# Hybrid layer on one core: banks of the down projection read by ScalarE, the residual added by transfers, and keys by token scaled ahead of the chains

## Chip, core and metric

The kernel runs on one core of a Trainium2 chip, in one launch. The metric is the device time of one execution in microseconds (us), lower is better. It took 1257.34 us, the median of three runs (1256.65 to 1259.51).

## What is computed

Input and output are 1024 tokens of 1024 floats. One layer has two mixers beside each other, a gated delta rule (4 heads) and a dilated windowed attention (8 heads), then an output projection, a gated MLP with a short convolution, and a last RMS norm. Cut to what matters here:

```python
h = rmsnorm(x, norm1_w);  proj = h @ w_in
# mixer A, per head and chunk: k is normed by l2norm, g = log decay, beta = sigmoid
k_end = kc * (jnp.exp(gc[..., -1:] - gc) * bc)[..., None]     # keys scaled by token
def step(state, xs):
    u = uv - jnp.einsum('bhck,bhkv->bhcv', wk, state)
    o = jnp.einsum('bhck,bhkv->bhcv', qd, state) + jnp.einsum('bhcj,bhjv->bhcv', at, u)
    state = ge[..., None, None] * state + jnp.einsum('bhck,bhcv->bhkv', ke, u)
    return state, o
x = x + jnp.concatenate([o_a, o_b], axis=-1) @ w_out
h = rmsnorm(x, norm2_w)
u = causal_dwconv(h @ w_up, ffn_conv_w)
gate, up = u[..., :D_FF], u[..., D_FF:]        # D_FF = 2816
x = x + (jax.nn.silu(gate) * up) @ w_down
return rmsnorm(x, final_norm_w)
```

## The kernel before

**Products.** Everything is float32. A product is made of three matmuls in the fp32r type (`mm3`, line 184): each operand is split into a high part (ScalarE, a copy that rounds) and a low part (VectorE, the difference), as in `split_block` (1052). So each operand of each product costs one ScalarE and one VectorE instruction. All matmuls have the line of `mm` (L177) in the profile and transposes that of `tp` (L181). All instructions of VectorE (DVE), ScalarE (ACT), GpSimd (POOL) and the transfers that SP issues have the line of the helper class `Engine` (L132), so groups are told apart by the names of their tiles.

**Order of the work.** The kernel is written as streams (Python generators: projections, keys, chains, attention, MLP), and a planner, `Weave` (lines 46 to 109), interleaves them. It keeps a modelled time of TensorE and of each engine, and resumes the stream that is due (`need` gives the delay after which a tile should be ready). Each TensorE instruction gets an order stamp, so TensorE keeps the planner's order; a scheduler places the instructions of the other engines by their data, so they may come earlier or later than their text. `after` (173) adds a wish on that order. A change of an operation's engine or cost in one stream can so move other streams' products.

**Keys of the delta rule** (`kprep`, 524; four heads, before 130 us). For each head, rows of log decay come into `dec`, ScalarE adds a bias in 8 instructions, GpSimd masks, ScalarE takes the exponential. TensorE transposes the keys `kT` to keys by token; `tokens` (505) copies them to `ktok` with ScalarE and adds up the squares of each chunk (`sq`, result `ssk`). From `ssk`, `beta` and `eg` come the 8 factors by chunk, `bp` and `ke`. Then TensorE multiplies keys by keys (`ps<-kT`), VectorE scales the result to `um`, which goes to the triangular solve.

**Chains** (`chain`, 730; four, from about 232 to 297 us, beside projection products). In a chunk, TensorE makes the 128x128 product `ps[:, P:2P]`; VectorE writes it scaled by `ke` into `wke`, and ScalarE copies it unscaled into `w`. `ktok` times `wke` gives the step of the state (read by VectorE), `at` times `w` the output.

**Down projection** (lines 1241 to 1411, from about 1027 us to the end). It is a Strassen-Winograd product of 2 x 2 halves: seven products of half size in four stages. Stages 0, 1 and 2 do two products each, stage 3 one. A stage has 11 steps j (`STEPS`, 1361), one for each pair of 128 rows of weights. A step multiplies four weight tiles of 128 columns by activations of 512 tokens for each product: into the four PSUM banks `pa` and the four `pb`, 24 matmuls in all. Banks accumulate over the steps, and partly over the stages. When a stage ends (j = 10) all eight banks are read: `add_to` (1329) lets VectorE add a bank to a half of an output row block `x1h[m]`, m = 0 to 7. `ADDS` (1364) says which. The first products of the next stage write the same banks. The step (1, 4) is step 4 of stage 1.

`prep` (1279) makes the operands of the next step while this one runs. SP loads raw weights (`wd`, `wa`, 512 and 256 KB). In stage 0 the activations come from `upark` in DRAM into `r1`. VectorE forms the weight sums in place, ScalarE and VectorE split them into tiles `pr`. The activations' sums T1 to T4 of the algorithm stay in `r1` and `r2`: T1 is formed in stage 0; T2 in a tile `t2` and T4 in stage 1; T3 in stage 2. `load_x1` (1315) loads the residual from `xpark` in 16 transfers of 256 KB on SP, at the steps in `XLOADS` (1362).

**Last norm.** `complete` (1333) squares a finished block on ScalarE and adds the squares to `rstdB` on VectorE. `final_norm` (1342) adds them over the partitions with matmuls against ones, takes the power on GpSimd, spreads it by transposes and scales eight blocks on VectorE, with a transfer of each to the output. `last_product` (1397) does the last five steps of stage 3 for one bank and half of its tokens at a time.

Of the kernel before, what the change touches and what calls it, by code (L numbers as in the profile page):

```python
# [135 lines left out]
def hybrid_layer(tc, I, out):  # L136
# [387 lines left out]
    def kprep(h):  # L524
# [29 lines left out]
        bp = small("bp", 4)  # L554
        ve.reciprocal(bp, ssk)
        ve.tensor_tensor(bp, bp, beta[:, :, h], op=OP.mult)
        ke = small("ke", 4)
        ve.tensor_tensor(ke, bp, eg, op=OP.mult)

        um = A("um", "uy", shape=(P, NCH, P))  # L560
        for c0 in range(0, NCH, 4):
# [12 lines left out]
        d.update(kT=kT, dec=dec, ge=ge, nk=nk, bp=bp, ke=ke, um=um)  # L574
        wv.done.add(("k", h))
        if all(("k", i) in wv.done for i in range(H)):
            forward_sub()
# [152 lines left out]
    def chain(h):  # L730
# [2 lines left out]
            yield from wv.until(("m", i))  # L733
            yield from wv.until(("v", i))
        d = G[h]
        kT, ktok, vtok, yt, ge, rq, gq, ke = [d[n] for n in ("kT", "ktok", "vtok", "yt", "ge", "rq", "gq", "ke")]
        if not ct:
            ct.append(A("ct", "uy", shape=(P, 8, P)))
        sts = ct[0][:, 2 * h:2 * h + 2, :]
# [5 lines left out]
        for c in range(NCH):  # L745
            cs = slice(c * P, (c + 1) * P)
            if c == 2 and h < 2:
                qb = chain_load(h, 1)
            if c == 3 and h >= 2:
                yield from wv.until(("c", h - 2, 3))  # L750
                qb = chain_load(h, 1)
            if c == 4:
                qa = qb
            qT, at = [qa[:, i, (c % 4) * P:(c % 4 + 1) * P] for i in range(2)]
            if c == 0:
                r = vtok[:, cs]
                yield wv.need(ps, vtok, yt)
            else:
                yield wv.need(ps, st, slack=HOP)
                mm(ps[:, 0:P], kT[:, cs], st, 0.215)  # L760
                r = tile_(sp, [P, P], F32, "r", "r" + tg, 1)
                ve.scalar_tensor_tensor(r, ps[:, 0:P], ngam[:, c, h:h + 1], vtok[:, cs], op0=OP.mult, op1=OP.add)
                yield wv.need(r, slack=HOP)
            mm(ps[:, P:2 * P], yt[:, c, :], r, 0.215)
            w = tile_(sp, [P, P], F32, "w", "w" + tg, 1)
            if c < NCH - 1:
                wke = tile_(sp, [P, P], F32, "wke", "r" + tg, 1)
                ve.tensor_scalar(wke, ps[:, P:2 * P], ke[:, c:c + 1], None, op0=OP.mult)
# [282 lines left out]

    def split_block(b, src):
        ac.activation(b[0], src, AF.Copy)
        ve.tensor_tensor(b[1], src, b[0].bitcast(F32), op=OP.subtract)

    def residual(m):

# [186 lines left out]
    x1h = {}  # L1244
    pcount = [0]
    LAST = 5

    def raw_tile(name, tag, src, n=2):
        t = tile_(wp, [P, n, 512], F32, name, tag, 2)
# [12 lines left out]
    def split_pair(src):  # L1262
# [4 lines left out]
        split_block((hi[0], lo[0]), src)  # L1267
        return [(hi[0][:, i, :], lo[0][:, i, :]) for i in range(2)]

    def split_one(src, tag=None):  # L1270
        if tag is None:
# [7 lines left out]
    def prep(stage, j):  # L1279
        if stage == 0:  # L1280

            g = raw_tile("wd", ("wst", "whi")[j % 2], wd_rows(j, 0))
            r = R1[j] = acts("r1", R1TAGS[j], j, 0)
            ops[stage, j] = list(zip(split_pair(g), split_pair(r)))
            q = R2[j] = A("r2", R2TAGS[j], shape=(P, 2, 512))
            sy.dma_start(q[:, 0, :], upark[j][:, half(1)])
            ve.tensor_tensor(r[:, 0, :], q[:, 0, :], r[:, 0, :], op=OP.subtract)
        elif stage == 1:

            u = raw_tile("wd", "wst", wd_rows(j, 1))  # L1290
            a = raw_tile("wa", "whi", wd_rows(j, 0)[:, 0:1], 1)
            r, q = R1[j], R2[j]
            sy.dma_start(q[:, 1, :], upark[HT + j][:, half(1)])
            t2 = tile_(wp, [P, 512], F32, "t2", "wlo", 2)
            ve.tensor_tensor(u[:, 1, :], u[:, 0, :], u[:, 1, :], op=OP.add)
            ve.tensor_tensor(u[:, 0, :], u[:, 1, :], a[:, 0, :], op=OP.subtract)
            ve.tensor_tensor(t2, q[:, 1, :], r[:, 0, :], op=OP.subtract)
            w = split_pair(u)
            ops[stage, j] = [(w[0], split_one(t2)), (w[1], split_one(r[:, 0, :]))]
            ve.tensor_tensor(r[:, 1, :], r[:, 1, :], t2, op=OP.subtract)  # L1300
        elif stage == 2:

            g = raw_tile("wd", "wst", wd_rows(j, 0))
            u = raw_tile("wd", "whi", wd_rows(j, 1))
            ve.tensor_tensor(g, g, u, op=OP.subtract)
            ve.tensor_tensor(g[:, 1, :], g[:, 0, :], g[:, 1, :], op=OP.add)
            r = R2[j]
            ve.tensor_tensor(r[:, 0, :], r[:, 1, :], r[:, 0, :], op=OP.subtract)
            ops[stage, j] = list(zip(split_pair(g), split_pair(r)))
        else:  # L1310

            a = raw_tile("wa", ("wst", "whi")[j % 2], wd_rows(j, 1)[:, 1:2], 1)
            ops[stage, j] = [(split_one(a[:, 0, :]), split_one(R1[j][:, 1, :], R2TAGS[j]))]

    def load_x1(mg, hh):
        for m in range(4 * mg, 4 * mg + 4):
            if not hh:
                x1h[m] = A("x1h", ("kT", "kT", "dv", "dv", "Xa", "Xa", "Xa", "Xa")[m])
            sy.dma_start(x1h[m][:, half(hh)], xpark[m][:, half(hh)])

    def down(pd, i, op, sl, first, last_):
        (whi, wlo), (hhi, hlo) = op
# [10 lines left out]
    def complete(m, hh, sl):  # L1333

        sp_ = part(m, hh, sl)
        x = x1h[m][:, sp_]
        sq = tile_(sp, [P, 512], F32, "sq3", "t2", 2)
        ac.activation(sq[:, sl] if m else rstdB[:, sp_], x, AF.Square)
        if m:
            ve.tensor_tensor(rstdB[:, sp_], rstdB[:, sp_], sq[:, sl], op=OP.add)  # L1340

    def final_norm(hh, sl, tags, between=None):
        n_ = (sl.stop - sl.start) // P
        ss = bank(tags[0])
        for c in range(n_):
            o = 512 * hh + sl.start + c * P
            mm(ss[:, c:c + 1], rstdB[:, o:o + P], ones[:, :1], 0.215)
# [8 lines left out]
        for m in range(8):  # L1356
            x = x1h[m][:, part(m, hh, sl)]
            ve.scalar_tensor_tensor(x, x, fw[:, m:m + 1], pb[:, :sl.stop - sl.start], op0=OP.mult, op1=OP.mult)
            sy.dma_start(out[m * P:(m + 1) * P, part(m, hh, sl)], x)

    STEPS = [(s_, j) for s_ in range(4) for j in range(HT)]
    XLOADS = {6: (0, 0), 12: (1, 0), 14: (0, 1), 16: (1, 1)}

    ADDS = (((0, 0), (0, 0)), ((0, 1), (1, 1)), ((1, 1), (0, 1)))

    def mlp_down():
        yield from wv.until("up")
# [3 lines left out]
        def down_step(stage, j):  # L1371
            for e, (op, pds) in enumerate(zip(ops[stage, j], (pa, pb))):
                for i in range(4):
                    down(pds[i], i, op, whole, j == 0 and (stage == 0 or (stage, e) == (1, 1)), j == HT - 1)
                if j == HT - 1:
                    mg, hh = ADDS[stage][e]
                    for i in range(4):
                        add_to(pds[i], 4 * mg + i, hh, whole)
                        if stage == 0 and e == 1:
                            complete(i, 0, whole)  # L1380
                        if stage == 2 and e == 1:
                            complete(i, 1, whole)
                    if stage == 2 and e == 1:
# [3 lines left out]
        for n, (stage, j) in enumerate(STEPS):  # L1387
            if n + 1 < len(STEPS):
                prep(*STEPS[n + 1])
            if n in XLOADS:  # L1390
                load_x1(*XLOADS[n])
# [5 lines left out]
        def last_product(i, sl):  # L1397
# [3 lines left out]
            complete(4 + i, 0, sl)  # L1401


        left, right = slice(0, 256), slice(256, 512)
# [81 lines left out]
```

## Time and profile before

| what | value |
|---|---|
| time, median of 3 runs | 1257.34 us |
| profiled execution: time, span | 1259.56 us, 1257.8 us |
| TensorE busy | 1233.0 us, 98% |
| VectorE busy | 936.0 us, 74% |
| ScalarE busy | 621.8 us, 49% |
| GpSimd busy | 47.8 us, 4% |
| mean granted TensorE clock | 0.993 |
| moved by transfers | 153.52 MB, mean 122 GB/s |

In the lines of the timeline, the first number is the start, the second the time from there to the end of the group, and the bracket tells how long the engine was idle before it and whose work ended that. In the list of waits, a row gives the sum, the number of times and the longest. In the windows, the numbers are the window's length, then the busy time and instruction count of TensorE, its weight loads, VectorE, ScalarE and GpSimd, then the granted clock, the share of the DMA engines and GB/s. A releaser is inferred, and a product that waits for several things is put down to the last.

### The profile page before, as it was taken

What the parts mean: (1) busy time and instruction counts of PE and PEld (TensorE: products, weight loads), DVE (VectorE), ACT (ScalarE), POOL (GpSimd) and SP (SyncE); (2) the same over time, 40 slices, a digit from 0 to 9 for tenths busy, and PEclk for the clock granted to TensorE, in tenths of its full rate; (3) what the DMA queues carried; (4) which work ended last, traced back from release to release, by engine and by line L of the source; (5) the groups of instructions that cost most, each with busy time, mean ns of one, the idle gap of its engine ahead of it and who ended that gap; (6) DMA issues with size and microseconds to landing.
All of it is one profiled execution on the core that took longest, in us unless ns stands there. A gap on an engine that the chain in (4) does not pass through costs nothing.

```text
span 1257.8 us, 18320 instructions
## 1 busy us (share of the span) xinstructions
PE 1233.0 (98%) x7040; PEld 1002.1 (80%) x7040; DVE 936.0 (74%) x1462; ACT 621.8 (49%) x1179; POOL 47.8 (4%) x34
## 2 busy tenths in 40 slices
PE   9989999999999999999999999999999999999996
PEld 7768887888676767878788888888888888787886
DVE  7566975563555455676798888888988989899875
ACT  7374444462757374465554454544544454343451
POOL 0021110022000000000000000000000000000000
PEclk9989999999999999999999999999999999999998
DMA  6313244255223420454312313223223298545523
GB/s 228 100 57 94 85 116 137 101 160 206 96 78 100 140 63 26 126 179 139 118 51 101 92 59 101 85 67 101 79 73 101 68 353 290 167 138 198 192 85 134
DMA packets 81974, 153.52 MB, mean 122 GB/s; under 512 B 21824, under 2 KB 32736, under 8 KB 81888
## 3 DMA queue, kind: packets, MB, share of 16 engines
q1 hardware_dynamic: 81888, 152.37, 37.1%
q8 instruction: 55, 0.90, 0.3%
q14 instruction: 31, 0.25, 0.1%
HBM read 114.31 MB, written 35.93 MB: 119 GB/s over the span
## 4 chain that ended last, share of the span: by engine, by line
PE 84%; DVE 7%; DMA 4%; ACT 2%; issue 2%; SPq 0%; POOL 0%; POOLq 0%; DVEq 0%; ACTq 0%
PE ps L177 44%; PE pa L177 18%; PE pc L177 9%; PE dw L177 8%; PE ps L181 4%; DMA wd<-in_wd 3%; DVE pr L132 2%; DVE x1h L132 1%; DVE wd L132 1%; ACT dec L132 1%; DVE kT L132 1%; PE warm L177 1%; DMA wst<-in_wu 0%; DVE r L132 0%; DVE xr L132 0%
## 5 line engine op out<-in xcount | busy, mean ns | idle before, releaser
L177 PE MATMUL dw<-pr 128*128 128x512 f32 (+1 forms) x984 | 213.3, 377 | 2.8 <-DVE x1h L132 2.8
L177 PEld LDWEIGHTS dw<-pr 128*128 128x128 f32 x984 | 176.1, 188 | 38.9 <-DVE x1h L132 4.9
L177 PE MATMUL ps<-xhi,whi 128*128 128x512 f32 x448 | 186.5, 416 | 0.0
L177 PE MATMUL ps<-xhi,wlo 128*128 128x512 f32 x448 | 175.8, 392 | 0.0
L177 PE MATMUL ps<-xlo,whi 128*128 128x512 f32 x448 | 175.3, 391 | 0.0
L177 PE MATMUL pa<-T,pair 128*128 128x512 f32 x528 | 127.1, 389 | 0.6 <-ACT u L132 0.6
L177 PEld LDWEIGHTS pa<-T,pair 128*128 128x128 f32 x528 | 99.0, 188 | 21.1 <-ACT u L132 0.7
L177 PEld LDWEIGHTS ps<-xhi,whi 128*128 128x128 f32 x448 | 84.6, 189 | 19.9 <-issue 6.0
L177 PEld LDWEIGHTS ps<-xhi,wlo 128*128 128x128 f32 x448 | 84.4, 188 | 18.5
L177 PEld LDWEIGHTS ps<-xlo,whi 128*128 128x128 f32 x448 | 84.8, 189 | 13.5
L132 ACT ACTIVATE sm<-sm,mx 128x512 f32<-128x512 f32 (+2 forms) x128 | 79.9, 651 | 23.0 <-DVE mx L132 23.0
L132 ACT ACTIVATE u<-pa 128x512 f32<-128x512 f32 x44 | 26.4, 600 | 110.5 <-PE pa L177 110.5
L132 DVE SCALAR_TENSOR_TENSOR y<-xu,fcw,y 128x1023 f32<-128x1023 f32 (+1 forms) x44 | 56.3, 1281 | 25.7 <-ACT y L132 25.7
L132 ACT ACTIVATE whi<-wst 128x1024 fp32r<-128x1024 f32 (+2 forms) x38 | 38.7, 1017 | 70.4 <-PE ps L177 63.0
L177 PE MATMUL pc<-B,pair 128*128 128x512 f32 x264 | 63.4, 389 | 0.0
L177 PE MATMUL pa<-B,A 128*128 128x512 f32 x264 | 63.4, 389 | 0.0
L177 PE MATMUL pc<-T,S 128*128 128x512 f32 x264 | 63.4, 389 | 0.0
L177 PE MATMUL pa<-T,S 128*128 128x512 f32 x264 | 63.4, 389 | 0.0
L132 ACT ACTIVATE pr<-wd 128x1024 fp32r<-128x1024 f32 x33 | 35.0, 1061 | 55.0 <-DVE wd L132 36.5
L132 DVE TENSOR_TENSOR wst<-wst 128x512 f32<-128x512 f32 x88 | 60.5, 687 | 0.7
L177 PE MATMUL ps<-B,pair 128*128 128x512 f32 x252 | 60.5, 389 | 0.0
L177 PEld LDWEIGHTS pc<-B,pair 128*128 128x128 f32 x264 | 49.6, 188 | 10.3
(230 smaller groups left out, 2279.8 us busy)
## 6 DMA issues: line engine op xcount, KB each, us to landing
wst<-in_wu SPq DMA_DIRECT2D x44, 512.0 KB, 3.7
wd<-in_wd SPq DMA_DIRECT2D x44, 512.0 KB, 4.3
wst<-in_wi SPq DMA_DIRECT2D x25, 512.0 KB, 3.7
upark<-y SPq DMA_DIRECT2D x22, 512.0 KB, 3.7
apark<-aqkv SPq DMA_DIRECT2D x12, 512.0 KB, 2.8
r<-upark SPq DMA_DIRECT2D x11, 512.0 KB, 7.6
r<-upark SPq DMA_DIRECT2D x22, 256.0 KB, 6.7
wa<-in_wd SPq DMA_DIRECT2D x22, 256.0 KB, 2.9
```

What stands on the lines that cost most here:

```text
L132: return getattr(eng, op)(*a, **kw)
L177: tc.stamp_issue_order_token(nc.tensor.matmul(dst, lhs, rhs, start=start, stop=stop, **kw).ins, TOKEN)
L181: tc.stamp_issue_order_token(nc.tensor.transpose(dst, src, ident).ins, TOKEN)
```

## The change

Five things change.

1. Down projection: at the ends of stages 0 and 1 ScalarE copies the banks into `x1h` (`copy_to`). The two products of stage 0 now go to two row blocks, `x1h[i]` and `x1h[4 + i]`, and `add_half` lets VectorE add the second to the first in steps 13 to 16. At the end of stage 2 VectorE adds banks as before.
2. The residual: `add_res` issues 12 transfers of 256 KB on GpSimd's queue that add a DRAM block to `x1h` in place (`accum_op`). Four plain loads by SP are left. The squares of the first four half blocks, once made at the end of stage 0, are made at steps 24 to 29 (`JOBS`), though the scheduler may place them earlier.
3. Activations' sums: stage 0 loads both halves of `r2` in one transfer and forms T3, and for j of 5 or more (`LATE`) T4. Stage 1 forms T2 in place, without the tile `t2`. Weight sums are asked to come behind the previous weights' split (`weight_sum`).
4. Last norm: the squares of the last two blocks are not added to `rstdB` but are summed by more matmuls into the same PSUM column (`more`).
5. Keys: `ktok` is scaled by `ke` once, by seven ScalarE instructions of 128x128 for each head. In the chain, VectorE copies the product into `w`, which both following products use; `wke` and ScalarE's copy are gone.

In the list of instructions, ScalarE has 756 rows in place of 778 and VectorE 1315 in place of 1306. TensorE's order is that of before up to 283 rows (the products up to the second head's keys), differs in how the projection's products lie between the third and fourth heads' key products, and is the same in the chains.

```diff
@@ kprep @@
-        ke = small("ke", 4)
+        ke = small("ke")
         ve.tensor_tensor(ke, bp, eg, op=OP.mult)
+        for c in range(NCH - 1):
+            ac.activation(v8(d["ktok"])[:, c, :], v8(d["ktok"])[:, c, :], AF.Copy, scale=ke[:, c:c + 1])
@@ chain @@
+            ve.tensor_copy(w, ps[:, P:2 * P])
             if c < NCH - 1:
-                wke = tile_(sp, [P, P], F32, "wke", "r" + tg, 1)
-                ve.tensor_scalar(wke, ps[:, P:2 * P], ke[:, c:c + 1], None, op0=OP.mult)
-            ac.activation(w, ps[:, P:2 * P], AF.Copy)
-            if c < NCH - 1:
-                yield wv.need(wke, slack=HOP)
-                mm(ps[:, 2 * P:3 * P], ktok[:, cs], wke, 0.215)
+                yield wv.need(w, slack=HOP)
+                mm(ps[:, 2 * P:3 * P], ktok[:, cs], w, 0.215)
@@ prep, stage 0 @@
-            ops[stage, j] = list(zip(split_pair(g), split_pair(r)))
-            q = R2[j] = A("r2", R2TAGS[j], shape=(P, 2, 512))
-            sy.dma_start(q[:, 0, :], upark[j][:, half(1)])
+            ops[stage, j] = list(zip(weight_pair(g), split_pair(r)))
+            q = R2[j] = acts("r2", R2TAGS[j], j, 1)
             ve.tensor_tensor(r[:, 0, :], q[:, 0, :], r[:, 0, :], op=OP.subtract)
+            ve.tensor_tensor(q[:, 0, :], q[:, 1, :], q[:, 0, :], op=OP.subtract)
+            if j >= LATE:
+                ve.tensor_tensor(r[:, 1, :], r[:, 1, :], q[:, 1, :], op=OP.subtract)
+                ve.tensor_tensor(r[:, 1, :], r[:, 1, :], r[:, 0, :], op=OP.add)
@@ prep, stage 1 @@
-            sy.dma_start(q[:, 1, :], upark[HT + j][:, half(1)])
-            t2 = tile_(wp, [P, 512], F32, "t2", "wlo", 2)
-            ve.tensor_tensor(u[:, 1, :], u[:, 0, :], u[:, 1, :], op=OP.add)
+            weight_sum(u[:, 1, :], u[:, 0, :], u[:, 1, :], op=OP.add)
             ve.tensor_tensor(u[:, 0, :], u[:, 1, :], a[:, 0, :], op=OP.subtract)
-            ve.tensor_tensor(t2, q[:, 1, :], r[:, 0, :], op=OP.subtract)
-            w = split_pair(u)
-            ops[stage, j] = [(w[0], split_one(t2)), (w[1], split_one(r[:, 0, :]))]
-            ve.tensor_tensor(r[:, 1, :], r[:, 1, :], t2, op=OP.subtract)
+            w = weight_pair(u)
+            t1 = split_one(r[:, 0, :])
+            ve.tensor_tensor(r[:, 0, :], q[:, 1, :], r[:, 0, :], op=OP.subtract)
+            ops[stage, j] = [(w[0], split_one(r[:, 0, :])), (w[1], t1)]
+            if j < LATE:
+                ve.tensor_tensor(r[:, 1, :], r[:, 1, :], r[:, 0, :], op=OP.subtract)
@@ prep, stage 2 @@
-            ve.tensor_tensor(r[:, 0, :], r[:, 1, :], r[:, 0, :], op=OP.subtract)
@@ new helpers @@
+    def weight_sum(*a, **kw):
+        inst = ve.tensor_tensor(*a, **kw)
+        if wlast[0] is not None:
+            after(inst, wlast[0], "raw weights are released before the next ones are waited for")
+    def add_res(mg, hh):
+        for m in range(4 * mg, 4 * mg + 4):
+            po_.dma_start(x1h[m][:, half(hh)], xpark[m][:, half(hh)], accum_op=OP.add)
+    def add_half(m):
+        x = x1h[m][:, half(0)]
+        in_turn(x, x, x1h[4 + m][:, half(0)])
+    def copy_to(pd, m, hh):
+        ac.activation(x1h[m][:, half(hh)], pd, AF.Copy)
@@ final_norm @@
+        parts = [rstdB[:, o:o + n_ * P]] + list(more)
+        for i, t in enumerate(parts):
+            for c in range(n_):
+                mm(ss[:, c:c + 1], t[:, c * P:(c + 1) * P], ones[:, :1], 0.215, i == 0 and c == 0,
+                   i == len(parts) - 1, skip_group_check=True)
@@ the order of the jobs @@
-    XLOADS = {6: (0, 0), 12: (1, 0), 14: (0, 1), 16: (1, 1)}
-    ADDS = (((0, 0), (0, 0)), ((0, 1), (1, 1)), ((1, 1), (0, 1)))
+    ADDS = (((0, 0), (1, 0)), ((0, 1), (1, 1)), ((1, 1), (0, 1)))
+    JOBS = {6: [(take_x1, 0)], 8: [(take_x1, 1)], 13: [(add_half, 0)], 14: [(add_half, 1)], 15: [(add_half, 2)],
+            16: [(add_half, 3)], 17: [(add_res, 0, 0)], 19: [(load_x1, 1, 0)], 24: [(add_res, 0, 1), (square, 0)],
+            25: [(square, 1)], 26: [(add_res, 1, 1)], 27: [(square, 2)], 29: [(square, 3)]}
@@ mlp_down @@
-                        add_to(pds[i], 4 * mg + i, hh, whole)
-                        if stage == 0 and e == 1:
-                            complete(i, 0, whole)
+                        if stage < 2:
+                            copy_to(pds[i], 4 * mg + i, hh)
+                        else:
+                            add_to(pds[i], 4 * mg + i, hh, whole)
@@ the end @@
-        for i in (2, 3):
-            last_product(i, right)
-        final_norm(0, right, ("hf", "ch"))
+        final_norm(0, right, ("hf", "ch"), more=[last_product(i, right, True) for i in (2, 3)])
```

More of the change, by code (lines that the diff above doesn't have):

```diff
@@ L573, in kprep @@
             sy.dma_start(md[r], um[b, :, b])
-        d.update(kT=kT, dec=dec, ge=ge, nk=nk, bp=bp, ke=ke, um=um)
+        d.update(kT=kT, dec=dec, ge=ge, nk=nk, bp=bp, um=um)
         wv.done.add(("k", h))
@@ L735, in chain @@
         d = G[h]
-        kT, ktok, vtok, yt, ge, rq, gq, ke = [d[n] for n in ("kT", "ktok", "vtok", "yt", "ge", "rq", "gq", "ke")]
+        kT, ktok, vtok, yt, ge, rq, gq = [d[n] for n in ("kT", "ktok", "vtok", "yt", "ge", "rq", "gq")]
         if not ct:
@@ L1053, in split_block @@
         ac.activation(b[0], src, AF.Copy)
-        ve.tensor_tensor(b[1], src, b[0].bitcast(F32), op=OP.subtract)
+        return ve.tensor_tensor(b[1], src, b[0].bitcast(F32), op=OP.subtract)
     def residual(m):
@@ L1246, in hybrid_layer @@
     LAST = 5
+    LATE = 5
     def raw_tile(name, tag, src, n=2):
@@ L1260, in acts, with weight_pair, split_pair @@
         return t
-    def split_pair(src):
+    wlast = [None]
+    def weight_pair(src):
+        pair, wlast[0] = split_pair(src, True)
+        return pair
+    def weight_sum(*a, **kw):
+        inst = ve.tensor_tensor(*a, **kw)
+        if wlast[0] is not None:
+            after(inst, wlast[0], "raw weights are released before the next ones are waited for")
+    def split_pair(src, inst=False):
         hi, lo = [], []
@@ L1266, in split_pair @@
             pcount[0] += 1
-        split_block((hi[0], lo[0]), src)
-        return [(hi[0][:, i, :], lo[0][:, i, :]) for i in range(2)]
+        lo_inst = split_block((hi[0], lo[0]), src)
+        pair = [(hi[0][:, i, :], lo[0][:, i, :]) for i in range(2)]
+        return (pair, lo_inst) if inst else pair
     def split_one(src, tag=None):
@@ L1304, in prep @@
             u = raw_tile("wd", "whi", wd_rows(j, 1))
-            ve.tensor_tensor(g, g, u, op=OP.subtract)
+            weight_sum(g, g, u, op=OP.subtract)
             ve.tensor_tensor(g[:, 1, :], g[:, 0, :], g[:, 1, :], op=OP.add)
-            r = R2[j]
-            ve.tensor_tensor(r[:, 0, :], r[:, 1, :], r[:, 0, :], op=OP.subtract)
-            ops[stage, j] = list(zip(split_pair(g), split_pair(r)))
+            ops[stage, j] = list(zip(weight_pair(g), split_pair(R2[j])))
         else:
@@ L1313, in prep, with take_x1, in_turn @@
             ops[stage, j] = [(split_one(a[:, 0, :]), split_one(R1[j][:, 1, :], R2TAGS[j]))]
+    def take_x1(mg):
+        for m in range(4 * mg, 4 * mg + 4):
+            x1h[m] = A("x1h", ("kT", "kT", "dv", "dv", "Xa", "Xa", "Xa", "Xa")[m])
     def load_x1(mg, hh):
         for m in range(4 * mg, 4 * mg + 4):
-            if not hh:
-                x1h[m] = A("x1h", ("kT", "kT", "dv", "dv", "Xa", "Xa", "Xa", "Xa")[m])
             sy.dma_start(x1h[m][:, half(hh)], xpark[m][:, half(hh)])
+    def in_turn(*a):
+        after(ve.tensor_tensor(*a, op=OP.add), wlast[0], "the next step's weights go first")
+    def add_res(mg, hh):
+        for m in range(4 * mg, 4 * mg + 4):
+            po_.dma_start(x1h[m][:, half(hh)], xpark[m][:, half(hh)], accum_op=OP.add)
+    def add_half(m):
+        x = x1h[m][:, half(0)]
+        in_turn(x, x, x1h[4 + m][:, half(0)])
     def down(pd, i, op, sl, first, last_):
@@ L1331, in add_to, with complete @@
         ve.tensor_tensor(x, x, pd[:, sl], op=OP.add)
-    def complete(m, hh, sl):
+    def complete(m, hh, sl, alone=False, turn=False):
         sp_ = part(m, hh, sl)
@@ L1338, in complete, with final_norm @@
         ac.activation(sq[:, sl] if m else rstdB[:, sp_], x, AF.Square)
+        if alone:
+            return sq[:, sl]
         if m:
-            ve.tensor_tensor(rstdB[:, sp_], rstdB[:, sp_], sq[:, sl], op=OP.add)
-    def final_norm(hh, sl, tags, between=None):
+            r = rstdB[:, sp_]
+            if turn:
+                in_turn(r, r, sq[:, sl])
+            else:
+                ve.tensor_tensor(r, r, sq[:, sl], op=OP.add)
+    def final_norm(hh, sl, tags, between=None, more=()):
         n_ = (sl.stop - sl.start) // P
         ss = bank(tags[0])
-        for c in range(n_):
-            o = 512 * hh + sl.start + c * P
-            mm(ss[:, c:c + 1], rstdB[:, o:o + P], ones[:, :1], 0.215)
+        o = 512 * hh + sl.start
+        parts = [rstdB[:, o:o + n_ * P]] + list(more)
[3 more added lines that the diff above has]
+                   i == len(parts) - 1, skip_group_check=True)
         rs = tile_(sp, [P, 4], F32, "rs3", "rs3", 2)
@@ L1359, in final_norm, with square @@
             sy.dma_start(out[m * P:(m + 1) * P, part(m, hh, sl)], x)
+    def square(m):
+        complete(m, 0, slice(0, 512), turn=True)
     STEPS = [(s_, j) for s_ in range(4) for j in range(HT)]
-    XLOADS = {6: (0, 0), 12: (1, 0), 14: (0, 1), 16: (1, 1)}
-    ADDS = (((0, 0), (0, 0)), ((0, 1), (1, 1)), ((1, 1), (0, 1)))
+    ADDS = (((0, 0), (1, 0)), ((0, 1), (1, 1)), ((1, 1), (0, 1)))
+    JOBS = {6: [(take_x1, 0)], 8: [(take_x1, 1)], 13: [(add_half, 0)], 14: [(add_half, 1)], 15: [(add_half, 2)],
+            16: [(add_half, 3)], 17: [(add_res, 0, 0)], 19: [(load_x1, 1, 0)], 24: [(add_res, 0, 1), (square, 0)],
+            25: [(square, 1)], 26: [(add_res, 1, 1)], 27: [(square, 2)], 29: [(square, 3)]}
     def mlp_down():
@@ L1377, in down_step @@
                     for i in range(4):
-                        add_to(pds[i], 4 * mg + i, hh, whole)
-                        if stage == 0 and e == 1:
-                            complete(i, 0, whole)
+                        if stage < 2:
+                            copy_to(pds[i], 4 * mg + i, hh)
+                        else:
+                            add_to(pds[i], 4 * mg + i, hh, whole)
                         if stage == 2 and e == 1:
@@ L1389, in mlp_down @@
                 prep(*STEPS[n + 1])
-            if n in XLOADS:
-                load_x1(*XLOADS[n])
+            for job, *a in JOBS.get(n, ()):
+                job(*a)
             if stage == 3 and j == HT - LAST - 1:
@@ L1395, in mlp_down, with last_product @@
                 down_step(stage, j)
-        def last_product(i, sl):
+        def last_product(i, sl, alone=False):
             for j in range(HT - LAST, HT):
@@ L1400, in last_product @@
             add_to(pa[i], 4 + i, 0, sl)
-            complete(4 + i, 0, sl)
+            return complete(4 + i, 0, sl, alone)
         left, right = slice(0, 256), slice(256, 512)
```

## The prediction

> **What bounds it now.** I read the engines' shares first, then TensorE's waits, then the windows and timelines of the places that they name. All numbers below are us of the profiled execution; it took 1259.56, 1257.8 of it in the span, 2.2 more than the median of the runs shown (1257.34).
>
> ```profile
> PE 1233.0 (98%) x7040; PEld 1002.1 (80%) x7040; DVE 936.0 (74%) x1462; ACT 621.8 (49%) x1179; POOL 47.8 (4%) x34
> ...
> PE   9989999999999999999999999999999999999996
> ```
> TensorE is busy 98% of the span, and the diff leaves its products as they are but for four matmuls of one column. So the change can save only idle TensorE time, about 25 in all, and only where it touches the cause. Who owns that time:
>
> ```profile
> PE ps L177 <- ACT sq L132: 5.0, 2, 4.4
> PE dw L177 <- DVE x1h L132: 2.8, 5, 1.1
> PE ps L177 <- DVE rstdB L132: 2.1, 1, 2.1
> ...
> PE ps L177 <- ACT w L132: 0.5, 1, 0.5
> ```
> Four of these rows stand where the diff works: keys by token (first row), the banks of the down projection (second), the last squares (third), the chains (fourth). The windows of the down projection's two stage ends say which engine is short there (columns: TensorE, weight loads, VectorE, ScalarE, GpSimd, clock, DMA share, GB/s):
>
> ```profile
> 1090.00:1120.00 30.00, 29.01 (x125) 23.36 (x126) 28.01 (x44) 11.77 (x18) 0.00 (x0) 1.00 0.58 193
> 1120.00:1150.00 30.00, 30.00 (x134) 24.81 (x133) 27.32 (x36) 12.92 (x18) 0.00 (x0) 1.00 0.60 190
> 1150.00:1180.00 30.00, 28.36 (x123) 22.63 (x122) 27.63 (x33) 13.64 (x16) 0.00 (x0) 1.00 0.53 180
> ```
> VectorE is full where TensorE loses time, ScalarE half idle. The wait itself at the second end:
>
> ```profile
> 1153.71 3.00 PE L177 MATMUL dw<-pr 128*128 128x512 f32 x12 [1.12 <-DVE x1h L132]
> 1157.23 0.98 PE L177 MATMUL dw<-pr 128*128 128x512 f32 x3 [0.52 <-DVE x1h L132]
> ```
>
> **Part 1, banks read by ScalarE.** Twelve matmuls take 2.72 here, 0.2267 each, so a step is 5.44 and a bank has 4.76 between its last product of one stage and its first of the next. VectorE must read eight banks in that time at 0.60 each (8 x 0.60 = 4.8) while splits and weight sums stand between. At the first end the waits are 0.33, 0.22 and 0.57; counted as matmuls missing against 0.2267, 1.9 is lost from 1087.7 to 1095. At the second they are 1.12 and 0.52, with 2.1 lost. In the changed kernel ScalarE reads these sixteen banks. The nearest row is its bank copy in the up projection, u<-pa 128x512, 0.600 (0.52 apart). Its order puts at most two splits (1.06 each by the timeline) between copies: 8 x 0.52 + 3 x 1.0 = 7.2 in the 8.2 from the first bank's end to the last bank's next use. The last of them can be held up by one split, which waits for VectorE's weight sum (2.65 idle before such a split at 1153.15). VectorE is without its 16 adds of 0.60, so its sums come earlier. I take both losses as gone, -1.9 - 2.1 = **-4.0**; bounds 0 and -4.0.
>
> **Part 2, what VectorE gets instead.** Six steps of stage zero get two adds of 0.60 each (T4), 1.2 a step of 5.44; stage one loses t2's slot and, for those steps, the T4 subtraction, 4.7 to 4.1 a step. Four sums of halves (0.60 each) lie in steps 13 to 16, where the adds of the banks used to be. The crowded place is 1030 to 1060 (VectorE 29.97 of 30, DMA share 0.98): In the timeline each split there ends 3 or more ahead of its product even with the added 1.2 a step. The order of instructions shows that the scheduler had put both R2 halves' loads and the T3 subtraction into stage zero already, so that part of the change is one of name. What does leave that stretch is eight loads of the residual, 256 KB each, from 1037 to 1056. Taken as **0**; if the cover of 3 were gone, a late split costs at most what it is late, bounds -0.3 to +1.
>
> **Part 3, the residual by accumulating transfers.** Twelve transfers of 256 KB are issued by GpSimd, which is otherwise idle from 620 to 1227. No run of before shows one of them. Nearest rows: 256 KB loads by SP land in 2.9 (wa, the page) and 1.8 to 7.5 (x1h). They bind at one place. The square of the first half block waits for its transfer, on ScalarE, ahead of the splits for step (1,4); the next two squares stand ahead of (1,5) and (1,6) in the same way. The half sum ends at about 1096.5, the transfer goes out at about 1097, ScalarE comes to the square at about 1100.6, and TensorE needs (1,4) at about 1109.9, with some 4 of splits before it. So a transfer may take 9 (issue to landing) at no cost. I take 3 to 7, from these rows: **0**. Beyond 9 every us late is a us of TensorE, at up to three places. The Trainium skill ("DMA: Bandwidth & Descriptors", Anatomy of one DMA — SWDGE (gpsimd) path) fits a transfer issued by GpSimd as about 2.0 us plus bytes over 436e3 per us, an estimate of 2.6 us here; no run of before shows that path, and the sum would stay at nothing for this part.
>
> **Part 4, keys scaled once.** ScalarE gets 28 scalings of 128x128; the row dec<-dec,ngc 128x128 x8 in 2.46 gives 0.295 each, 2.1 a head. The chains lose 28 wke of 0.344 on VectorE and 32 w<-ps of 0.278 on ScalarE, and gain 32 copies on VectorE; off the path, except that the state product waited for one operand and w for the other engine's copy. In the chains the matmuls lose 0.63 (0.47 of it ACT w), 0.22, 0.84 and 0.41; one VectorE hop in place of two takes the first and perhaps another: **-1.0**, bounds 0 and -2.0. In exchange ScalarE is nearly full where the scalings fall (the window, TensorE's wait there, and ScalarE's queue after it):
>
> ```profile
> 60.00:90.00 30.00, 25.01 (x117) 20.72 (x116) 21.81 (x42) 27.07 (x86) 8.30 (x6) 0.89 0.18 57
> ```
> ```profile
> 71.35 1.86 PE L177 MATMUL ps<-kT 128*128 128x128 f32 x7 [4.42 <-ACT sq L132]
> ```
> ```profile
> 78.27 0.21 ACT L132 ACTIVATE eg<-gend 128x8 f32<-128x8 f32 x1 [0.25 <-DVE ke L132]
> 79.51 1.06 ACT L132 ACTIVATE dec<-dec 128x1024 f32<-128x1024 f32 x1 [1.03 <-POOL dec L132]
> ```
> The window has a granted clock of 0.89; after the wait of 4.42 in the second fence it is half for 6.83. TensorE's order is the same up to this wait, so it stays. The first head's seven scalings stand behind the tanh of kT at 78, in front of dec's exp and the next ktok: 2.1, of which the idle 0.25 and 1.03 absorb 1.3. TensorE's order now has 18 instead of 9 projection products ahead of the third head's key products, so these come at about 88.6, and the wait of 0.57 at 87.19 (0.74 with its ramp) goes. A new one of 0.4 is possible at about 100, where a weight split is behind the second head's scalings. **-0.3**, bounds -0.7 and +3. The Trainium skill ("TensorE: Matmul & The Clock Gate", Part 1: The HAM clock gate) says that the array falls to half clock after one idle window of about 3.4 us. The trace agrees: a wait of 4.42 us, then a granted clock of one half for 6.83 us.
>
> **Part 5, the last squares.** The kernel ends with
>
> ```profile
> 1246.72 0.95 DVE L132 TENSOR_TENSOR rstdB<-rstdB,sq 128x256 f32<-128x256 f32 x2 [0.21 <-ACT sq L132]
> ...
> 1247.82 0.98 PE L177 MATMUL ps<-ones,rstdB 128*128 128x1 f32 x4 [2.10 <-DVE rstdB L132]
> ```
> The last products end at 1245.72. Two sums, 0.95, leave the path; the matmuls take the squares themselves. The last square is there at about 1247.0 instead of the sum at 1247.67, and the extra matmuls of the earlier parts run while TensorE waits: **-0.7**, bounds -0.3 and -1.0.
>
> **Sum.** -4.0 + 0 + 0 - 1.0 - 0.3 - 0.7 = -6.0: 1259.56 - 6.0 = 1253.56 on the profiled execution, and 1257.34 - 6.0 = 1251.34 on the median; I say **1251.5**. With the bounds of parts 1 to 5 added up the ends are -8.0 and +3.7, that is 1249.3 and 1261.0, but they will hardly all fall on one side.
>
> **The rivals.**
> - *The gain is eaten.* A ScalarE stall at the keys of 0.9 (2.1 - 1.3, and a queue behind it) sits after a stretch at half clock; if it draws another such stretch, that is 6.83 x 0.5 = 3.4 more. Or the copies come late at one stage end and half of the 4.0 stays. -6.0 + 4.3 gives about 1255.6. For it: ScalarE 27.07 of 30. Against it: the 0.74 that leaves by the new product order.
> - *Slower: the accumulating transfers.* If such a transfer needs 12.5 instead of 3 to 7, the squares hold ScalarE and the splits of three steps are 3.5 late each, 10.5 in all, with no half clock counted: -6.0 + 10.5 = +4.5, 1261.8. It decides from a landing of 9. For it: no row shows one, and 256 KB took up to 7.5 on the crowded queue. Against it: at 1097 to 1110 the DMA engines are at 0.58. The Trainium skill ("SBUF — State Buffer", the "DVE blocks DMA" trap) says that VectorE in its two-port modes, as an fp32 copy within SBUF, keeps GpSimd from writing the descriptors of its transfers; VectorE is at 28 of 30 here, but with sums of two tensors. No run of before shows it.
> - *It does not do what it says.* The moves of T3 and R2 are in the old order already; if the banks' stalls also stay, since each read then waits for ScalarE's split instead of VectorE's, only parts 4 and 5 are left: -2.0, 1255.3. I count it with the first rival.
> - *More.* The waits at 615 and the rest of the chains' losses shrink too, or stage two's VectorE runs ahead: 1246 to 1249.
>
> **Chances.** Forecast, 1249 to 1254.7: 0.55. Gain eaten or not there, around 1255.5, 1254.8 to 1259.8: 0.20. Slower by the transfers or the keys, around 1262: 0.15. More, 1246 to 1249: 0.10. About 0.2% (2.5) is what a measurement of this kernel can tell from no change. So faster 0.65, the same 0.20, slower 0.15. The range leaves out most of the slower case and the far end of the larger gain: 1247 to 1259.5.
>
> **What would show it.** Right: the row of waits for DVE x1h loses its 2.8 with no row for ACT x1h of over 0.5 in its place; windows 1090 to 1120 and 1150 to 1180 show TensorE at 29.9; the accumulating transfers land within 9; the wait at 1247.82 falls from 2.10 to about 1.4; the chains' row for ACT w is gone. Wrong: a wait for DVE or ACT pr between 1105 and 1125, a clock below 1.00 there, a wait for ACT in 78 to 105 that draws the clock down again.

## The result, and the profile after

The changed kernel took 1261.52 us (median of 20 runs; 1259.01 for the kernel before in the same job). The ratio is 1.0024, 95% interval 1.0017 to 1.0031: about 3 us slower. One of the 20 runs, of 1485.37 at a granted clock of 0.777, is left out of the ratio. The forecast was 1251.5, faster by some 6.

The profiled execution has a span of 1261.8, against 1257.8. It took 1263.92, 2.4 above the median, at a mean granted clock of 0.989; the 18 other runs of the ratio had 0.988 to 0.995, so lost clock weighs more in this profile than in most of them. TensorE's own waits, in the view that the prediction began with (sum, times, longest):

```profile
PE ps L177 <- ACT sq L132: 4.5, 2, 4.4
PE dw L177 <- DVE pr L132: 3.8, 3, 2.4
PE ps L177 <- DVE vtok L132: 2.4, 1, 2.4
...
PE ps L177 <- DVE rstdB L132: 0.3, 1, 0.3
```
The wait for `DVE x1h` (2.8) is gone, as forecast, and so are those for `ACT w` (0.5) and most of that for `rstdB` (2.1). In their place stand 3.8 for splits of the down projection (`DVE pr`) and 2.4 for `vtok` in the chains. The window of the chains in the kernel before, and then the windows of the changed kernel (same columns as before):

```profile
240.00:300.00 60.00, 58.27 (x397) 52.29 (x396) 36.86 (x113) 33.56 (x126) 13.61 (x8) 1.00 0.44 144
```

```profile
240.00:300.00 60.00, 57.18 (x383) 51.92 (x382) 37.32 (x114) 27.24 (x95) 10.60 (x6) 0.94 0.41 136
...
1090.00:1120.00 30.00, 28.92 (x128) 23.61 (x127) 27.72 (x39) 14.83 (x25) 2.81 (x3) 1.00 0.66 184
1120.00:1150.00 30.00, 30.00 (x134) 24.83 (x133) 24.42 (x33) 13.44 (x20) 1.41 (x2) 1.00 0.60 181
1150.00:1180.00 30.00, 27.55 (x115) 22.38 (x114) 22.15 (x25) 16.58 (x23) 6.48 (x8) 0.94 0.85 226
```
At 1150 to 1180 VectorE is not full any more (22.15, before 27.63), and yet TensorE loses more; the DMA share has gone from 0.53 to 0.85, and the clock is at 0.94. The chains' window has lost clock too, 0.94 in place of 1.00.

TensorE's progress, from the starts of the same products in three profiles. `best` is the last kernel of the experiments:

| stretch, us | before | changed | best |
|---|---|---|---|
| start to the first product of the triangular solve | 188.63 | 188.70 | 188.00 |
| from there to the first product of the up projection: chains, attention, output projection | 416.05 | 418.62 | 414.42 |
| from there to the first product of the down projection | 423.49 | 424.72 | 424.95 |
| down projection, to the end of its last product | 217.55 | 219.04 | 213.62 |
| from there to the end | 12.08 | 10.72 | 10.71 |
| span | 1257.8 | 1261.8 | 1251.7 |

The third stretch holds no edit; its 1.2 to 1.5 are granted clock at 616 to 624 (12 matmuls in 4.6 us in place of 3.0), which comes and goes between profiles.

**The chains.** VectorE's queue in the changed kernel, then GpSimd's:

```profile
270.00 2.89 DVE L132 TENSOR_TENSOR wlo<-wst,whi 128x1024 fp32r<-128x1024 f32 x1
272.81 0.34 DVE L132 SCALAR_TENSOR_TENSOR vtok<-ps,gq,vtok 128x128 f32<-128x128 f32 x1
```
```profile
269.92 1.90 POOL L132 TENSOR_TENSOR vtok<-vtok,ms 128x1024 f32<-128x1024 f32 x1
```
The same pair in the kernel before, VectorE and then GpSimd:

```profile
270.95 1.21 DVE L132 TENSOR_TENSOR wlo<-wst,whi 128x1024 fp32r<-128x1024 f32 x1
```
```profile
271.07 2.85 POOL L132 TENSOR_TENSOR vtok<-vtok,ms 128x1024 f32<-128x1024 f32 x1
```
Here whoever starts second takes about 1 to 1.7 us longer. Before, the split of a projection weight came first by 0.12 and GpSimd's product, for which TensorE did not wait, was stretched. In the changed kernel the chains' VectorE work is shorter, GpSimd's product starts 0.08 ahead of the split, and the split takes 2.89. Behind it on VectorE stands the `vtok` that TensorE needs:

```profile
273.21 0.80 PE L177 MATMUL ps<-ct,qat 128*128 128x128 f32 x2 [2.35 <-DVE vtok L132]
```
The Trainium skill ("SBUF — State Buffer", SBUF: two separate sides) says just this: a VectorE instruction with two inputs in SBUF and a GpSimd instruction that reads SBUF take a shared pair of ports as an exclusive lock, and whichever starts first keeps it for the whole instruction. The traces agree, 2.89 in place of 1.21 on the one side, 2.85 in place of 1.90 on the other.

**The second stage end.** GpSimd's queue, TensorE's, and the chain of work that ended last:

```profile
1149.45 7.12 POOL L132 DMA_DIRECT2D x1h<-xpark  x8 [27.67 <-ACT x1h L132]
```
```profile
1166.83 3.64 PE L177 MATMUL dw<-pr 128*128 128x512 f32 x8 [2.45 <-DVE pr L132]
```
```profile
1154.43 9.89 DMA wd<-in_wd
```
Eight accumulating transfers go out within 7 us, as soon as ScalarE has copied the banks: steps 24 and 26 of `JOBS` bind only the place in the text, and nothing else is on GpSimd's queue. The weights for step (2,2), issued at 1154.43, land 9.89 later (median of such loads in the kernel before: 4.3), and TensorE waits 2.45 and then goes at half clock. Counted as in the prediction, by the starts of the same matmuls against 0.2267 us each, the changed kernel loses 4.3 here and 1.4 near 1115. The kernel before loses 2.0 and 2.3 at its two stage ends, and these losses are gone.

### The profile page after: what moved, and what is told of

The parts are those of the page before. It is cut to its first block, busy times and chain, and to the rows that moved or that the text cites. A ratio compares the mean times of both kernels' runs of the same rounds, so it can differ in the third digit from the quotient of the medians.

```text
span 1261.8 us, 18342 instructions
## 1 busy us (share of the span) xinstructions
PE 1237.3 (98%) x7048; PEld 1008.1 (80%) x7048; DVE 935.1 (74%) x1458; ACT 629.9 (50%) x1191; POOL 57.4 (5%) x46
## 5 line engine op out<-in xcount | busy, mean ns | idle before, releaser
L132 ACT ACTIVATE pr<-r 128x512 fp32r<-128x512 f32 (+1 forms) x55 | 43.3, 795 | 54.6 <-DVE pr L132 21.7
L132 DVE TENSOR_TENSOR aqkv<-ps,rstdB 128x512 f32<-128x512 f32 x24 | 26.4, 1099 | 46.1 <-PE ps L177 46.1
```

Source lines behind the costliest of these rows:

```text
L132: return getattr(eng, op)(*a, **kw)
```

## The experiments

Each ratio is against the kernel before in the same job, with its 95% interval; 0.001 is 1.26 us.

**1. `keys_only`: the kernel before with the change's fifth item alone** (the diff's hunks of `kprep` and `chain`; the expectations call it part 5, the prediction part 4).

> The kernel before with part 5 alone (keys by token scaled once, VectorE copies w). Theory A (a lock): the chains lose 3.0 us, because GpSimd's product vtok<-vtok,ms starts just ahead of VectorE's split wlo<-wst,whi and holds it (2.89 us in place of 1.23 in the changed kernel's trace), TensorE waits 2.35 for vtok and the clock drops; keys -0.35. Sum +2.6 us against before, and a split of over 2.5 us near 270. Theory B (the chain's new order on VectorE is itself slower, or the scalings cost ScalarE): about +2.6 too, but with every split at 1.2 and the loss spread over several small waits. If neither: -1.3 us, as predicted at first (chains -1.0, keys -0.3).

Measured: 0.9997 (0.9986 to 1.0009). The split near 270 takes 2.88 and TensorE waits 2.35 for `vtok`, as theory A had it. But the stretch from the solve to the up projection is 417.25, +1.2 against before and not +3.0: the clock of the window is 0.97 instead of 0.94, half for about 3.4 us instead of 6.8. The keys' stretch is 0.2 shorter in spite of a start that was 0.8 later, but that is in part luck: behind the wait of 4.4 for the keys the clock was half for 3.4 us in this profile and for 6.83 in those of the kernel before and the changed one. So the mechanism is there, and the size by which I had tied it to the result was too large for this kernel.

**2. `down_only`: the changed kernel without these hunks.**

> The changed kernel with part 5 undone: only the down projection and the last norm change. By the two traces the down projection costs +1.5 and the end gives -1.4, so +0.1 us against before; TensorE's waits for DVE pr of about 1.1 near 1115 and 2.4 near 1165 stay, the clock there stays below 1.00, and the chains are those of before. If the loss were a consequence of the chains' (later start, another phase), the down projection would be -4 us and the whole -5.4.

Measured: 1.0004 (0.9994 to 1.0013), +0.5 us. The down projection takes 218.82 and the end 10.5, with waits of 1.57 near 1111 and of 1.62 and 1.00 at 1162 and 1168, so its loss does not come from the chains. The clock stayed at 1.00 there, where I had expected less. The two parts alone add up to nothing, together to 3 us. The traces show one place for it: after the same wait of 2.35 in the chains the clock was half for 6.8 us in the changed kernel and for 3.4 in `keys_only`, and after the waits near 1165 only in the changed kernel. Over all runs in the ratios the mean granted clock was 0.9927 for the changed kernel, 0.9936 for `keys_only`, 0.9941 for `down_only` and 0.9940 for the kernel before beside these two; 0.0013 of 1260 us is 1.6, an estimate of what clock took of the 3. The rest stays open.

**3. `pieces`: GpSimd's product in eight.**

```diff
-        po_.tensor_tensor(v8(vtok), v8(vtok), ms[:, :, None].to_broadcast([P, NCH, P]), op=OP.mult)
+        for c in range(NCH):
+            x = vtok[:, c * P:(c + 1) * P]
+            po_.tensor_tensor(x, x, ms[:, c:c + 1].to_broadcast([P, P]), op=OP.mult)
```

> The changed kernel, with GpSimd's product vtok<-vtok,ms (128x1024, 1.90 us) cut into eight of 128x128. Theory A (lock): no VectorE instruction can be held for longer than one piece (some 0.3 us), the split takes at most 1.6 in place of 2.89, TensorE's wait of 2.35 near 272 and the clock drop go: -2.5 to -3.0 us against the changed kernel, equal to before. Theory B (VectorE's order): the wait of 2.35 stays and the time is that of the changed kernel.

Measured: 1.0043 (1.0031 to 1.0056), slower. The split took 1.39 and the wait fell to 0.85, by theory A. But the planner, charged for eight instructions, laid TensorE's order in another way, and the attention lost 3.63 to a wait for `ACT sm` that takes 0.74 in the changed kernel. So this kernel couldn't tell by its time.

**4. `pieces_same`: the same, with the planner charged as for one.**

```diff
+        wv.account("gpsimd", 0.15 + 0.0021 * 1024, [vtok], [vtok, ms], 0.28)
         for c in range(NCH):
             x = vtok[:, c * P:(c + 1) * P]
-            po_.tensor_tensor(x, x, ms[:, c:c + 1].to_broadcast([P, P]), op=OP.mult)
+            nc.gpsimd.tensor_tensor(x, x, ms[:, c:c + 1].to_broadcast([P, P]), op=OP.mult)
```

> The changed kernel with GpSimd's product vtok<-vtok,ms in eight pieces, but with the planner charged for it as before, so that TensorE's order is that of the changed kernel (the earlier run with pieces also had another order, and lost 3.6 us to a wait for ACT sm in the attention). Theory A (lock): the split wlo<-wst,whi near 270 takes at most 1.5 in place of 2.89, TensorE's wait for vtok near 272 falls from 2.35 to about 0.85, with no clock drop after it: -1.5 to -3.3 us against the changed kernel. Theory B (VectorE's order in the chain): the split is short, but the wait stays over 2 and the time with it.

Measured: 1.0005 (0.9996 to 1.0014), 2.4 us under the changed kernel's 1.0024. VectorE and TensorE of this kernel:

```profile
268.96 1.39 DVE L132 TENSOR_TENSOR wlo<-wst,whi 128x1024 fp32r<-128x1024 f32 x1
```
```profile
270.67 0.49 PE L177 MATMUL ps<-ct,qat 128*128 128x128 f32 x2 [0.85 <-DVE vtok L132]
```
Theory A holds. The 0.85 that is left is the split's own length ahead of `vtok`, as the 0.67 before.

**5. `spread`: the last eight accumulating transfers one to a step.**

```diff
+    def add_one(m, hh):
+        inst = po_.dma_start(x1h[m][:, half(hh)], xpark[m][:, half(hh)], accum_op=OP.add)
+        tc.add_manual_dep(inst.ins, wlast[0].ins.name, sync, reason="one transfer a step")
...
-            24: [(add_res, 0, 1), (square, 0)],
-            25: [(square, 1)], 26: [(add_res, 1, 1)], 27: [(square, 2)], 29: [(square, 3)]}
+            24: [(add_one, 0, 1), (square, 0)],
+            25: [(square, 1), (add_one, 1, 1)], 26: [(add_one, 2, 1)], 27: [(square, 2), (add_one, 3, 1)],
+            28: [(add_one, 4, 1)], 29: [(square, 3), (add_one, 5, 1)], 30: [(add_one, 6, 1)], 31: [(add_one, 7, 1)]}
```

(`sync` makes the transfer wait for the weights' low split `wlast` with a semaphore; `after` only sets an order within an engine's queue.)

> The changed kernel, with the last eight accumulating transfers one to a step: each waits for the weights' low split of its step, in place of all eight going out at 1149 to 1156. Theory C (burst): the weight load of step (2,2) lands in about 4.5 in place of 9.9 us, TensorE's wait of 2.45 for DVE pr near 1165 and the half clock after it go: -3.5 to -3.9 us against the changed kernel. Rival D (ScalarE is late by its bank copies and squares): the wait near 1165 stays at over 1.5 although the load lands early, and the gain is under 1 us. The wait of 1.1 near 1115 stays by both.

Measured: 0.9983 (0.9974 to 0.9991), 5.2 us under the changed kernel. The window answers to the third above:

```profile
1150.00:1180.00 30.00, 30.00 (x134) 24.86 (x133) 26.06 (x28) 17.41 (x22) 2.57 (x3) 1.00 0.65 185
```
No wait in this window, full clock, with ScalarE's copies where they were. Theory C holds, rival D falls. The ratio's 5.2 is more than the 3.5 to 3.9 expected, and not all of it is shown to be the burst. By the profiles the 4.3 lost at step (2,2) are gone, but the wait near 1113 grew from 1.08 to 1.85 and one of 0.76 came near 1185, so the down projection is 2.5 shorter (216.51 against 219.04). The rest of the 5.1 between the two spans lies in stretches that this edit leaves alone.

**6. `spread_sq`: with it, the squares behind the splits of steps 24 to 29.** `whigh` is ScalarE's last high split. In the changed kernel ScalarE stood before the first two squares as follows:

```profile
1108.30 0.63 ACT L132 ACTIVATE rstdB<-x1h 128x512 f32<-128x512 f32 x1 [1.30 <-DMA x1h<-xpark]
1114.96 0.63 ACT L132 ACTIVATE sq<-x1h 128x512 f32<-128x512 f32 x1 [2.00 <-DMA x1h<-xpark]
```

```diff
+        if turn:
+            after(inst, whigh[0], "squares come behind the splits of this step")
```

> The kernel with spread transfers, and the squares of the first four half blocks put behind ScalarE's splits of steps 24 to 29, when their transfers have long landed. Theory E (ScalarE's squares wait for the first four accumulating transfers ahead of the splits of stage one): the wait of 1.85 for DVE pr near 1113 goes, -1.8 to -2.3 us against the kernel with spread transfers. Rival F (VectorE itself is late there by the half sums and the in-place T2): the wait stays at over 1, and the gain is under 0.7.

Measured: 0.9973 (0.9964 to 0.9983), 1.3 us less; the intervals overlap. The wait near 1112 falls from 1.85 to 0.95, so about half of it was theory E. The other half fits rival F: by the chain of waits VectorE is the last link from 1099 on, at 5.96 a step.

**7. `all_fixed`: the edits of 4, 5 and 6 together.**

> Spread transfers, late squares and pieces with the planner charged as before, together. If theories A, C and E hold: no TensorE wait of over 0.9 in the chains and none of over 0.5 from 1028 to 1200; 1260.0 (before) - 4.0 (bank waits) - 1.0 (end) - 0.5 (keys) + 0.3 (chain) = some 5 us under before, ratio 0.996. If one fails, the ratio stays at 0.998 or above.

Measured: 0.9959 (0.9947 to 0.9970), 5.2 us faster than the kernel before. The wait of 0.95 near 1110 is still there.

**8. `dve_copies`: kernel 6 with the bank copies on VectorE.**

```diff
-        ac.activation(x1h[m][:, half(hh)], pd, AF.Copy)
+        ve.tensor_copy(x1h[m][:, half(hh)], pd)
```

> The kernel with spread transfers and late squares, with its sixteen bank copies on VectorE instead of ScalarE. Theory G (the waits at the two stage ends of before come from VectorE's load): the waits come back, for DVE x1h or DVE pr, 2 to 4 us in all against the kernel with the copies on ScalarE. Rival H (ScalarE's copies bring nothing; VectorE has room since the sums have left it): the same time within 1 us.

Measured: 1.0026 (1.0015 to 1.0037), 6.7 us over kernel 6, more than either theory gave. In the profiles the down projection differs by 4.0 (219.74 against 215.75); the other 2.7 of the ratio is not in that stretch and stays open. The waits for `pr` grow from 1.6 to 3.6, in five places, the longest 2.11 at 1114. Theory G holds: the banks' reads on VectorE are what cost time.

**9. `best`: kernel 7 with the sums of halves in steps 17 to 20.**

```diff
-    13: [(add_half, 0)], 14: [(add_half, 1)], 15: [(add_half, 2)], 16: [(add_half, 3)], 17: [(add_res, 0, 0)], 19: [(load_x1, 1, 0)],
+    17: [(add_half, 0)], 18: [(add_half, 1)], 19: [(add_half, 2)], 20: [(add_half, 3), (add_res, 0, 0)], 21: [(load_x1, 1, 0)],
```

> The kernel all_fixed, with the four sums of halves in steps 17 to 20 instead of 13 to 16, and the plain loads behind them. Theory I (VectorE is over its step in steps 13 to 16: sums of halves beside T4, which stage one still forms for j under 5, 5.96 us a step against TensorE's 5.44): the wait of 0.95 for DVE pr near 1111 goes, -0.9 to -1.2 us against all_fixed, ratio about 0.995. Rival: the wait only moves to the later steps, same time as all_fixed.

Measured: 0.9961 (0.9949 to 0.9973); its median is 1252.71 us, the least of all kernels. The window has no wait left,

```profile
1090.00:1120.00 30.00, 30.00 (x134) 24.86 (x133) 26.91 (x39) 12.03 (x18) 0.17 (x1) 1.00 0.48 140
```
as theory I has it. The first four transfers and the plain loads moved along with the sums, so this run alone can't part VectorE's load from theirs; that VectorE was the last link stands in the chain of kernel 6. The 1 us that it gives in the profile is below what the ratios of kernels 7 and 9 can tell apart.

**10. `best_nokeys`: kernel 9 without the hunks of `kprep` and `chain`, and with GpSimd's product whole.**

> The kernel best without part 5 (keys scaled in the chain as before, GpSimd's product whole). It tells what part 5 is worth once nothing holds the split: by the traces (keys -0.4, chains +0.2) it is within 0.7 us of best; by the prediction it would be 1.3 us slower than best. Against before: the down projection and the end alone, -4.0 - 1.0 = -5 us, ratio 0.996.

Measured: 0.9971 (0.9959 to 0.9984), 1.3 us over `best` by the ratios, though the intervals overlap. By the profiles, the keys and chains save 2.2 up to the up projection (604.59 against 602.42), 0.3 of it an earlier start. This has the sign of the prediction's -1.3, and it is more than the 0.2 that I made of the first traces; by the ratios it is not clear of the noise.

**11. `burst_late`: kernel 9 with the eight transfers in one burst in mid stage.**

```diff
+            25: [(square, 1)], 27: [(square, 2)] + [(add_one, m, 1) for m in range(8)], 29: [(square, 3)]}
```

> The kernel best, with the last eight accumulating transfers in one burst again, but in the middle of stage two (step 27) instead of at its start. Theory C (a burst of 2 MB delays the weights' load, wherever it is): a weight load of over 8 us and a TensorE wait of 1.5 to 3 for DVE pr or wd near 1185, +2 to +4 us against best. Rival D (the burst hurt only because it met ScalarE's copies at the stage end): within 0.7 us of best.

Measured: 0.9989 (0.9978 to 0.9999), 3.5 us over `best`. TensorE, and the transfers between 1170 and 1195 (size, median us to landing):

```profile
1191.27 8.97 PE L177 MATMUL dw<-pr 128*128 128x512 f32 x31 [2.25 <-DVE pr L132]
```
```profile
wd<-in_wd SPq DMA_DIRECT2D x7, 512.0 KB, 8.3
x1h<-xpark POOLq DMA_DIRECT2D x8, 256.0 KB, 11.7
```
and in `best`, where they go out one by one:

```profile
wd<-in_wd SPq DMA_DIRECT2D x7, 512.0 KB, 5.0
x1h<-xpark POOLq DMA_DIRECT2D x5, 256.0 KB, 5.8
```
The stall went with the burst to a place without any bank copy. Theory C holds there too: the down projection is 3.6 longer than that of `best` (217.22 against 213.62).

## Why the prediction was wrong, step by step

The forecast gains were there; what failed is what I had priced at nothing.

- **Part 1 (-4.0), right.** The waits for `x1h` went and no wait for ScalarE came; the down projection of `best` is 3.9 shorter than before. One figure of its sum was off, to no harm: from the first bank's end to the last bank's next use lie 42 matmuls of 0.2267, 9.5 us, not 8.2.
- **Part 2 (0), wrong in one place.** "Four sums of halves lie in steps 13 to 16, where the adds of the banks used to be": in these steps stage one still forms T4 (j under 5), so a step of VectorE takes 5.96 against TensorE's 5.44. I had taken the relief of the later steps (4.1) for the whole stage. About 1 us.
- **Part 3 (0), the step that failed most.** "They bind at one place" was said of all twelve transfers, and only the first four were costed. Their landing I had right (4.7 to 6.3 us, within 3 to 7). Their issue I had wrong: the half sum is bound behind the next weights' low split, 1102.20 and not 1096.5, so the first transfer left at 1103.54, and ScalarE waited 1.30 and 2.00 for the first two landings. That was the slower rival's mechanism, by a late issue and not a slow landing, at 1.3 us instead of 10; that its 1261.8 lies near the measured 1261.5 is luck. The eight others I didn't price at all. I looked only at who waits for these transfers, and not at what they do to the transfers beside them: 5.2 us by the ratio, 4.3 by the matmuls of the trace, the largest item. The order of instructions gave it away: on GpSimd's queue nothing stands between the bank copies and the eight issues.
- **Part 4, keys (-0.3), right:** 0.3 after taking off the later start (188.70 - 7.59 against 188.63 - 7.17). **Chains (-1.0), wrong in the changed kernel:** +2.6, by the split that GpSimd's product held. I had costed GpSimd as off the path. With that taken away the stretch is 1.6 shorter than before.
- **Part 5 (-0.7), right in sign:** 1.4 by the profile, of which up to 0.8 may be clock, since the same code took 12.08 in the kernel before and 11.3 in `keys_only`.
- **Half clock, left out of the sum:** the prediction counted it for one rival at the keys alone, behind the one wait in the trace that had drawn it (4.42). Waits of about half that length drew it too: see the last section.

From the ratios: the burst 5.2, the lock 2.4, the squares 1.3 make 8.9, and the changed kernel stands 9.0 from the forecast (+3.0 against -6.0). That these agree so well is in part luck: removed together, in `all_fixed`, they give 8.2. `best`, with all of them removed, stands at -4.9 (-6.4 to -3.4).

## What to carry to other kernels

A transfer that nothing waits for still has a price: ask what else is in flight when it is issued, and hold a batch back with a real dependency, since its place in the program only sets its order on a queue that may be empty. An engine off the path can hold one on it, as GpSimd's product held the split here; which one waited hung on starts about 0.1 us apart, so any change of timing ahead of such a pair can turn it round, and cutting the long instruction in pieces bounded the harm (1.39 in place of 2.89). When work is moved to other steps, add up the engine's time in just those steps, not in the stage.

## What the runs showed of the hardware

- Waits of 2.09 to 2.45 us were mostly followed by half clock here: after 2.35 in the chains of the changed kernel the granted clock was 0.50 from 274 to 278, after 2.25 in `burst_late` 0.50 from 1193 to 1195, after 2.09 in `pieces` 0.50. Waits of 1.85 (`spread`) and 2.11 (`dve_copies`) were followed by 1.00. Near 620 the changed kernel's clock was half behind a wait of only 0.58, which came after matmuls of one column. The Trainium skill ("TensorE: Matmul & The Clock Gate", Part 1: The HAM clock gate) puts it at one idle window or more, about 3.4 us; these runs show it after shorter waits too.
- An accumulating transfer of 256 KB from GpSimd's queue lands in 5.5 to 5.8 us (medians) when it goes out alone, and in 10.1 and 11.7 in the two batches of eight. The late batch moved the median of the loads beside it from 5.0 to 8.3.
- GpSimd's product of 128x1024 takes 1.90 in one piece, and eight pieces of 128x128 beside VectorE take 3.88 (`pieces_same`).
